# When the first loads start and how the last one arrives: two edits at the ends of a batched matrix product

## The chip, the core and the metric

The kernel runs on one core of a Trainium2 chip. The metric is device time in microseconds (us) for one execution; lower is better. The kernel before took 138.43 us (median of 4 runs, 138.32 to 138.64).

A core has a matrix engine (TensorE, PE in the profile), a vector engine (VectorE, DVE), a scalar engine (ScalarE, ACT), a general engine (GpSimd, POOL) and a synchronisation engine (SyncE, SP). Data moves between device memory and the core's own memory by DMA, on 16 DMA engines that all queues of the core share. A DMA is issued by an instruction of SyncE, ScalarE or GpSimd, and each of these three has a queue of its own: in the trace, queue 1 is SyncE's, queue 10 ScalarE's and queue 0 GpSimd's.

## The reference: what is computed

```python
a = randn(1024, 64, 64)   # float32
b = randn(1024, 64, 64)   # float32
out = matmul(a, b)        # float32, 1024 products of 64 x 64 matrices
```

The kernel reads 16.78 MB of a and as much of b, and writes 16.78 MB of output.

## The kernel before

The 1024 products are cut into 16 b tiles of 64 products (index t, 0 to 15) and 8 a tiles of 128 products (index s = t // 2, 0 to 7). The products are made in bf16 and summed in float32. Each a matrix must be transposed, and several small matrices are put into one 128 x 128 block for the matrix engine.

The work on a: `load_a(s)` (L62) issues four DMAs from GpSimd, one for each quarter h. They turn float32 into bf16 on the way: 512 KB are read and 256 KB written by each. `regroup(s)` (L76) reorders the tile on VectorE. `transpose(s, w)` (L83) makes 16 transposes on the matrix engine against the 128 x 128 tile `identity`, then copies them out of the accumulators, one half on VectorE (L94) and one on ScalarE (L96). `spread(t)` (L98) copies the blocks with four VectorE instructions into a block-diagonal tile, of which there are two, cleared once at the start (L164).

The work on b: `load_b(t)` (L70) issues one DMA of 1 MB for tiles 0 to 14, from ScalarE for t = 1 and 3, else from SyncE. `cast(t)` (L108) turns the tile into bf16 with one ScalarE instruction (L111). For the last tile, t = 15, there is no load into float32: `cast(15)` issues four GpSimd DMAs (L115) that turn float32 into bf16 on the way, 256 KB read and 128 KB written by each. The last b tile is called b15 from here on, the one before it b14.

The product: `multiply(t)` (L122) has four parts (gq). Each makes 16 matrix instructions (L144) and then copies one accumulator to the output tile, on ScalarE (L156), or for the last tile on VectorE where gq is odd (L154). `store(t)` (L118) issues the output's DMA from GpSimd: 1 MB in one piece (L134), but four pieces of 256 KB for the last tile (L128). It is called one step of the loop late (`HOLD = 2`), so that store(t - 1) stands behind multiply(t) in the order of the program.

The order of work on each engine is the order of the calls: the whole is under a manual schedule, and each engine runs its instructions as they are written, waiting where data or a buffer is missing. At the start:

```python
load_a(0)
for t in range(B_AHEAD):      # B_AHEAD = 4
    load_b(t)
...                           # two memsets
make_identity(nc, identity)   # two GpSimd instructions, after load_a(0)
for s in range(1, A_AHEAD):   # A_AHEAD = 3
    load_a(s)
```

`make_identity` is a library helper (masks.py): it fills the tile with zeros (a memset on GpSimd) and then writes ones on the diagonal (one GpSimd selection).

Buffers: three a tiles, four float32 b tiles, two of each working tile, five output tiles. Tile t of b therefore takes the buffer of tile t - 4 and waits for that tile's cast; a product waits for an output tile until the store five steps earlier has landed. At the end of each step of the loop come `cast(t + 1)`, `load_b(t + 4)` and `store(t - 1)` in this order, so GpSimd meets the four DMAs of `cast(15)` ahead of store 13.

Of the kernel before, what the change touches and what calls it, by code (L numbers as in the profile page):

```python
# [7 lines left out]

fp32 = mybir.dt.float32
# [4 lines left out]
def kernel(  # L14
# [3 lines left out]
    b: bass.AP,  # L18
    out: bass.AP,
):  # L20

# [3 lines left out]
    nc = tc.nc  # L28
# [4 lines left out]
    n_t, n_s = B // 64, B // 128  # L33
    A_AHEAD = 3
    B_AHEAD = 4
# [4 lines left out]
    b_v = b.rearrange("(t g h) (kp u) n -> t (h kp) g (u n)", h=4, g=16, u=2)  # L40
# [16 lines left out]
    ]  # L57
    identity = consts.tile([128, 128], bf16)
    a_tiles, b_tiles, abf_tiles, at_tiles, bbf_tiles = {}, {}, {}, {}, {}
    held = {}  # L60

    def load_a(s):  # L62
        a_sb = a_pool.tile([128, 4, 16, 64], bf16, name="a_sb")
        for h in range(4):
            nc.gpsimd.dma_start(  # L65
                out=a_sb[:, h, :, :].rearrange("p v k -> p (v k)"), in_=a_v[s, h]
            )
        a_tiles[s] = a_sb

    def load_b(t):  # L70
        b_sb = b_pool.tile([128, 16, 128], fp32, name="b_sb")
        queue = nc.scalar if t in (1, 3) else nc.sync
        queue.dma_start(out=b_sb[:], in_=b_v[t])  # L73
        b_tiles[t] = b_sb

    def regroup(s):  # L76
        a_sb = a_tiles.pop(s)
        a_bf = work.tile([128, 16, 4, 64], bf16, name="a_bf")
        nc.vector.tensor_copy(a_bf[:], a_sb[:].rearrange("p h v k -> p v h k"))  # L79
        abf_tiles[s] = a_bf  # L80
        at_tiles[s] = work.tile([128, 2, 2, 128, 8], bf16, name="at_sb")

    def transpose(s, w):  # L83
        a_cols = abf_tiles[s][:].rearrange("p v h k -> p v (h k)")
        for u in range(2):
            at_ps = t_psum.tile([128, 8, 128], bf16, name="at_ps")
            for vo in range(8):
                nc.tensor.transpose(  # L88
                    at_ps[:, vo, :], a_cols[:, 2 * vo + w, u::2], identity[:]
                )  # L90
            dst = at_tiles[s][:, w, u, :, :]
            src = at_ps[:].rearrange("p vo q -> p q vo")
            if u == 0:
                nc.vector.tensor_copy(dst, src)  # L94
            else:
                nc.scalar.copy(dst, src)  # L96

    def spread(t):  # L98
        at_v = at_tiles[t // 2][:].rearrange(
            "p w u (g mp) vo -> p (w u) g (mp vo)", g=32  # L100
        )
        half = slice(16 * (t % 2), 16 * (t % 2) + 16)
        bd_v = bd_tiles[t % N_BD][:].rearrange("p (wu g) h mo -> p wu g h mo", g=16)
        for h in range(4):
            rows = slice(32 * h, 32 * h + 32)
            nc.vector.tensor_copy(bd_v[rows, :, :, h, :], at_v[rows, :, half, :])  # L106

    def cast(t):  # L108
        b_bf = work.tile([128, 16, 128], bf16, name="b_bf")
        if t < n_t - 1:  # L110
            nc.scalar.copy(b_bf[:], b_tiles.pop(t)[:])  # L111
        else:
            for gq in range(4):
                rows = slice(4 * gq, 4 * gq + 4)
                nc.gpsimd.dma_start(out=b_bf[:, rows, :], in_=b_v[t, :, rows, :])  # L115
        bbf_tiles[t] = b_bf

    def store(t):  # L118
        for piece in held.pop(t):
            piece()  # L120

    def multiply(t):  # L122
        at_bd, b_bf = bd_tiles[t % N_BD], bbf_tiles.pop(t)
        last = t == n_t - 1
        o_sb = o_pool.tile([128, 4, 4, 2, 64], fp32, name="o_sb")

        def put(gq):
            nc.gpsimd.dma_start(  # L128
                out=o_v[t, :, 4 * gq : 4 * gq + 4, :],
                in_=o_sb[:, gq, :, :, :].rearrange("p g w n -> p (g w n)"),  # L130
            )

        def put_all():
            nc.gpsimd.dma_start(  # L134
                out=o_v[t], in_=o_sb[:].rearrange("p q g w n -> p (q g w n)")
            )

        for gq in range(4):
            o_ps = o_psum.tile([128, 4, 2, 64], fp32, name="o_ps")
            for g4 in range(4):  # L140
                g = 4 * gq + g4
                for w in range(2):
                    for u in range(2):
                        nc.tensor.matmul(  # L144
                            o_ps[:, g4, w, :],
                            at_bd[:, (2 * w + u) * 16 + g, :, :].rearrange(
                                "p h mo -> p (h mo)"
                            ),
                            b_bf[:, g, 64 * u : 64 * u + 64],
                            start=(u == 0),  # L150
                            stop=(u == 1),
                        )
            if last and gq % 2:
                nc.vector.tensor_copy(o_sb[:, gq, :, :, :], o_ps[:])  # L154
            else:
                nc.scalar.copy(o_sb[:, gq, :, :, :], o_ps[:])  # L156
        held[t] = [lambda q=q: put(q) for q in range(4)] if last else [put_all]

    with tc.manual_schedule():
        load_a(0)  # L160
        for t in range(B_AHEAD):
            load_b(t)
        for bd in bd_tiles:
            nc.vector.memset(bd[:], 0.0)  # L164
        make_identity(nc, identity)
        for s in range(1, A_AHEAD):
            load_a(s)
        regroup(0)
        transpose(0, 0)
        transpose(0, 1)  # L170
        spread(0)
        cast(0)
        regroup(1)
        load_a(A_AHEAD)
        transpose(1, 0)
        for t in range(n_t):
            s, half = t // 2, t % 2
            if t + 1 < n_t:
                spread(t + 1)
            if half == 0:  # L180
                if s + 2 < n_s:
                    regroup(s + 2)
                if s + 1 + A_AHEAD < n_s:
                    load_a(s + 1 + A_AHEAD)
            multiply(t)
            if t + 1 < n_t:
                cast(t + 1)
            if t + B_AHEAD < n_t - 1:
                load_b(t + B_AHEAD)
            if half == 0 and s + 1 < n_s:  # L190
                transpose(s + 1, 1)
            if half == 1 and s + 2 < n_s:
                transpose(s + 2, 0)
            if t >= HOLD - 1:
                store(t - HOLD + 1)
        for t in range(n_t - HOLD + 1, n_t):
            store(t)
# [30 lines left out]
```

## Time and profile before

| | |
|---|---|
| median of 4 runs | 138.43 us |
| the profiled execution | 138.32 us |
| its span, first to last instruction | 136.5 us |
| granted matrix clock, mean | 0.841 |
| queue 0 (GpSimd: a, stores, b15) | 25.69 MB, 70.4% of 16 engines' span |
| queue 1 (SyncE: b) | 13.63 MB, 28.4% |
| queue 10 (ScalarE: b1, b3) | 2.10 MB, 4.2% |
| b tiles from SyncE, issue to landing | 22.4 us, median |
| a quarters, issue to landing | 16.3 us, median |
| stores of 1 MB, issue to landing | 21.2 us, median |
| b15's pieces, issue to landing | 8.4 us, median |
| first regroup of a starts at | 16.77 us |
| last copy out of the accumulators starts at | 126.89 us |

All times within the profile count from the start of the span. The megabytes of a queue are counted on the writing side, so a load that turns float32 into bf16 counts for half of what it reads. The rows of a window of time give the busy time of PE, PEld (weight loads), DVE, ACT and POOL, each with its number of instructions, then the granted clock of the matrix engine, the mean busy share of the 16 DMA engines and the rate of their writes. A DMA share over 1 means that packets overlap on an engine. In the timeline each line has the start, the duration, the engine, the line of the kernel, the operation, what is written and read, and in brackets how long the engine had been idle and what ended that.

### The profile page before, as it was taken

The numbers are of one execution on the slowest core, as the hardware profiler recorded it, in microseconds if no ns is written. First come the engines' busy times: TensorE is split into PE (matmuls) and PEld (weight loads), VectorE is DVE, ScalarE is ACT, GpSimd is POOL, SyncE is SP. The second block draws the span as 40 slices with busy tenths as digits, with TensorE's granted clock in tenths as the row PEclk, the third lists the DMA queues.
The fourth block names the chain that finished last, engine by engine and source line by source line (L and its number), as shares of the span: only waits on it lengthen the run. The fifth ranks groups of instructions, "written<-read, shape, count | busy, mean of one in ns | idle before, by whom it ended". The sixth has DMA issues, their size and how long they took to land.

```text
span 136.5 us, 2992 instructions
## 1 busy us (share of the span) xinstructions
PE 58.8 (43%) x1280; PEld 56.5 (41%) x1280; DVE 83.7 (61%) x92; ACT 76.8 (56%) x96; POOL 47.3 (35%) x61
## 2 busy tenths in 40 slices
PE   0000073196854684470497206680085716078100
PEld 0000072195854684470497106580085715077100
DVE  5770067889699999998179803995058908802200
ACT  1120018158999999915976078830979767355100
POOL 6811142354245503451132734300203122914700
PEclk9999999658999999999658965899658996558965
DMA  2999999999999999999999999999999999999993
GB/s 86 305 304 311 304 275 259 209 246 274 242 251 290 378 283 269 331 380 366 279 269 353 376 360 271 269 369 383 382 380 379 383 384 383 377 246 312 295 282 97
DMA packets 19053, 41.61 MB, mean 305 GB/s; under 512 B 3168, under 2 KB 3168, under 8 KB 19040
## 3 DMA queue, kind: packets, MB, share of 16 engines
q0 software_dynamic: 11120, 25.69, 70.4%
q1 hardware_dynamic: 6864, 13.63, 28.4%
q10 hardware_dynamic: 1056, 2.10, 4.2%
q8 instruction: 10, 0.16, 0.5%
q14 instruction: 3, 0.02, 0.0%
HBM read 33.55 MB, written 16.78 MB: 369 GB/s over the span
## 4 chain that ended last, share of the span: by engine, by line
DMA 52%; SPq 12%; issue 9%; POOL 6%; ACT 6%; PE 5%; DVE 4%; POOLq 1%; DVEq 0%; ACTq 0%
DMA a_sb<-in_a_dram 21%; DMA b_sb<-in_b_dram 17%; DMA out_dram<-o_sb 15%; SPq L73 12%; ACT o_sb L156 3%; PE o_ps L144 3%; PE at_ps L88 3%; POOL b_bf L115 2%; DVE a_bf L79 2%; DVE at_bd L106 2%; POOL out_dram L134 2%; ACT at_sb L96 1%; POOL a_sb L65 1%; ACT b_bf L111 1%; POOL out_dram L128 1%
## 5 line engine op out<-in xcount | busy, mean ns | idle before, releaser
L144 PE MATMUL o_ps<-b_bf,at_bd 128*128 128x64 bf16 x1024 | 40.9, 208 | 44.9 <-ACT b_bf L111 44.4
L106 DVE COPY at_bd<-at_sb 32x2048 bf16<-32x2048 bf16 x64 | 46.0, 719 | 22.2 <-ACT at_sb L96 21.2
L144 PEld LDWEIGHTS <-at_bd 128*128 128x128 bf16 x1024 | 40.0, 108 | 46.7 <-issue 36.9
L156 ACT COPY o_sb<-o_ps 128x512 f32<-128x512 f32 x62 | 33.9, 620 | 22.1 <-DMA out_dram<-o_sb 15.5
L65 POOL DMA_DIRECT2D a_sb<-in_a_dram x32 | 20.6, 649 | 37.2 <-DMA a_sb<-in_a_dram 26.0
L134 POOL DMA_DIRECT2D out_dram<-o_sb x15 | 19.7, 1316 | 38.8 <-ACT o_sb L156 20.8
L111 ACT CAST b_bf<-b_sb 128x2048 bf16<-128x2048 f32 x15 | 29.1, 1943 | 4.9 <-DMA b_sb<-in_b_dram 4.9
L88 PE MATMUL at_ps<-identity,a_bf 128*128 128x128 bf16 x256 | 20.2, 244 | 23.2 <-DVE a_bf L79 23.2
L88 PEld LDWEIGHTS <-a_bf 128*128 128x128 bf16 x256 | 17.8, 111 | 23.4 <-DVE a_bf L79 23.4
L96 ACT COPY at_sb<-at_ps 128x1024 bf16<-128x1024 bf16 x16 | 16.9, 1054 | 17.2 <-PE at_ps L88 17.2
L94 DVE COPY at_sb<-at_ps 128x1024 bf16<-128x1024 bf16 x16 | 19.5, 1221 | 4.5 <-PE at_ps L88 4.4
L79 DVE COPY a_bf<-a_sb 128x4096 bf16<-128x4096 bf16 x8 | 10.3, 1294 | 7.6 <-DMA a_sb<-in_a_dram 7.4
L164 DVE MEMSET at_bd<- 128x4096 uint32 x2 | 6.9, 3472 | 2.5 <-PEq L212 1.7
L154 DVE COPY o_sb<-o_ps 128x512 f32<-128x512 f32 x2 | 1.4, 692 | 7.1 <-PE o_ps L144 7.1
L115 POOL DMA_DIRECT2D b_bf<-in_b_dram x4 | 3.3, 833 | 5.3 <-ACT o_sb L156 5.3
L96 ACT ACT_TABLE_LOAD x1 | 1.3, 1283 | 4.1 <-issue 4.1
L128 POOL DMA_DIRECT2D out_dram<-o_sb x4 | 3.0, 755 | 0.0
L73 ACT MOVE_SHAPE b_sb<-in_b_dram x2 | 0.6, 320 | 1.6 <-issue 0.9
masks.py:199 POOL TENSOR_SCALAR_AFFINE_SELECT identity<-identity 128x128 bf16<-128x128 bf16 x1 | 0.3, 289 | 0.1
masks.py:197 POOL MEMSET identity<- 128x128 bf16 x1 | 0.3, 267 | 0.0
L212 POOL MEMSET const-float32-0.0<- 128x1 f32 x1 | 0.1, 99 | 0.2 <-issue 0.2
L212 POOL MEMSET const-bfloat16-1.0<- 128x1 bf16 x1 | 0.1, 102 | 0.0
(2 smaller groups left out, 0.2 us busy)
## 6 DMA issues: line engine op xcount, KB each, us to landing
out_dram<-o_sb POOLq DMA_DIRECT2D x15, 1024.0 KB, 21.2
a_sb<-in_a_dram POOLq DMA_DIRECT2D x32, 256.0 KB, 16.3
out_dram<-o_sb POOLq DMA_DIRECT2D x4, 256.0 KB, 6.9
b_bf<-in_b_dram POOLq DMA_DIRECT2D x4, 128.0 KB, 8.4
b_sb<-in_b_dram SPq DMA_DIRECT2D x13, 0.5 KB, 22.4
b_sb<-in_b_dram ACTq DMA_DIRECT2D x2, 0.5 KB, 18.2
```

What stands on the lines that cost most here:

```text
L65: nc.gpsimd.dma_start(out=a_sb[:, h, :, :].rearrange("p v k -> p (v k)"), in_=a_v[s, h])
L73: queue.dma_start(out=b_sb[:], in_=b_v[t])
L79: nc.vector.tensor_copy(a_bf[:], a_sb[:].rearrange("p h v k -> p v h k"))
L88: nc.tensor.transpose(at_ps[:, vo, :], a_cols[:, 2 * vo + w, u::2], identity[:])
L94: nc.vector.tensor_copy(dst, src)
L96: nc.scalar.copy(dst, src)
L106: nc.vector.tensor_copy(bd_v[rows, :, :, h, :], at_v[rows, :, half, :])
L111: nc.scalar.copy(b_bf[:], b_tiles.pop(t)[:])
L134: nc.gpsimd.dma_start(out=o_v[t], in_=o_sb[:].rearrange("p q g w n -> p (q g w n)"))
L144: nc.tensor.matmul(o_ps[:, g4, w, :], at_bd[:, (2 * w + u) * 16 + g, :, :].rearrange("p h mo -> p (h mo)"), b_bf[:, g, 64 * u : 64 * u + 6 ...
L156: nc.scalar.copy(o_sb[:, gq, :, :, :], o_ps[:])
L164: nc.vector.memset(bd[:], 0.0)
```

## The change

The change has two edits.

At the start, the fill of `identity` with zeros moves into `load_a(0)`, between the first of its four DMAs and the second. The loads of b tiles 0 and 1 get an added dependency on that fill, so that SyncE and ScalarE issue them after it; b tiles 2 and 3 stand behind them on the same two engines. The selection that writes the diagonal stays where it was, now written out instead of in the helper.

At the end, `load_b` is called for t = 15 as for the others, so that b15 is loaded in float32 by SyncE, into the buffer of tile 11. Its cast to bf16 is done in four instructions of 512 columns each: parts 0 and 2 on ScalarE, parts 1 and 3 on VectorE. The four GpSimd DMAs of `cast(15)` are gone.

```diff
     def load_a(s):
         a_sb = a_pool.tile([128, 4, 16, 64], bf16, name="a_sb")
         for h in range(4):
+            if s == 0 and h == 1:
+                begun.append(nc.gpsimd.memset(identity[:], 0.0))
             nc.gpsimd.dma_start(
                 out=a_sb[:, h, :, :].rearrange("p v k -> p (v k)"), in_=a_v[s, h]
             )
...
         queue = nc.scalar if t in (1, 3) else nc.sync
-        queue.dma_start(out=b_sb[:], in_=b_v[t])
+        load = queue.dma_start(out=b_sb[:], in_=b_v[t])
+        if t < 2:
+            tc.add_manual_dep(
+                load.ins,
+                begun[0].ins.name,
+                mybir.DependencyInfo(
+                    mybir.DependencyClass.Sync, mybir.DependencyReason.DATA
+                ),
+                reason="first load of a goes ahead",
+            )
...
         b_bf = work.tile([128, 16, 128], bf16, name="b_bf")
+        b_sb = b_tiles.pop(t)
         if t < n_t - 1:
-            nc.scalar.copy(b_bf[:], b_tiles.pop(t)[:])
+            nc.scalar.copy(b_bf[:], b_sb[:])
         else:
             for gq in range(4):
                 rows = slice(4 * gq, 4 * gq + 4)
-                nc.gpsimd.dma_start(out=b_bf[:, rows, :], in_=b_v[t, :, rows, :])
+                if gq % 2:
+                    nc.vector.tensor_copy(b_bf[:, rows, :], b_sb[:, rows, :])
+                else:
+                    nc.scalar.copy(b_bf[:, rows, :], b_sb[:, rows, :])
...
-        make_identity(nc, identity)
+        nc.gpsimd.affine_select(
+            out=identity[:],
+            in_=identity[:],
+            compare_op=mybir.AluOpType.not_equal,
+            fill=1.0,
+            base=0,
+            pattern=[[-1, 128]],
+            channel_multiplier=1,
+        )
...
-            if t + B_AHEAD < n_t - 1:
+            if t + B_AHEAD < n_t:
                 load_b(t + B_AHEAD)
```

More of the change, by code (lines that the diff above doesn't have):

```diff
@@ L5 @@
 from concourse import bass_utils, mybir
-from concourse.masks import make_identity
 from concourse._compat import with_exitstack
@@ L59 @@
     a_tiles, b_tiles, abf_tiles, at_tiles, bbf_tiles = {}, {}, {}, {}, {}
-    held = {}
+    held, begun = {}, []
     def load_a(s):
```

## The prediction

> **What bounds the kernel now.** I read the page's slices first. The DMA row stands at 9 from the second slice to the last but one: the sixteen DMA engines, not a compute engine, are full for the whole run.
>
> ```profile
> span 136.5 us, 2992 instructions
> PE 58.8 (43%) x1280; PEld 56.5 (41%) x1280; DVE 83.7 (61%) x92; ACT 76.8 (56%) x96; POOL 47.3 (35%) x61
> DMA  2999999999999999999999999999999999999993
> HBM read 33.55 MB, written 16.78 MB: 369 GB/s over the span
> ```
>
> Then busy time by window (the last two columns are the DMA share and GB/s counted on the writing side), at the start and at the end, where the change acts.
>
> ```profile
> 0.00:2.39 2.39, 0.00 (x0) 0.00 (x0) 0.72 (x1) 0.64 (x2) 1.30 (x6) 1.00 0.00 0
> 2.39:4.76 2.37, 0.00 (x0) 0.00 (x0) 2.37 (x1) 0.00 (x0) 2.30 (x7) 1.00 0.96 310
> 4.76:16.00 11.24, 0.00 (x0) 0.00 (x0) 3.85 (x2) 1.28 (x1) 3.17 (x6) 1.00 1.08 303
> ...
> 96.00:108.00 12.00, 7.12 (x155) 7.00 (x155) 6.70 (x9) 11.02 (x16) 2.31 (x2) 0.72 1.03 381
> ...
> 117.50:119.50 2.00, 0.00 (x0) 0.00 (x0) 1.58 (x3) 1.15 (x1) 2.00 (x3) 0.50 1.03 387
> 119.50:126.00 6.50, 5.34 (x112) 4.97 (x111) 0.62 (x1) 3.68 (x6) 1.59 (x3) 0.67 1.36 280
> ...
> 128.00:134.00 6.00, 0.00 (x0) 0.00 (x0) 0.00 (x0) 0.00 (x0) 0.94 (x2) 0.72 0.99 281
> ```
>
> Nothing moves before 2.39. With b loads and stores mixed, 381 GB/s pass. From 128 to 134 only stores are left, and they pass at 281, although stores alone ran at 387 for the short stretch from 117.5. The last 10 us are thus a drain of finished output: the compute engines are done at 127.6.
>
> Last the timeline, which gives the order of issue at both ends.
>
> ```profile
> 0.79 0.85 ACTq L73 DMA_DIRECT2D b_sb<-in_b_dram  x1
> 0.80 2.49 SPq L73 DMA_DIRECT2D b_sb<-in_b_dram  x2
> 1.30 2.33 POOL L65 DMA_DIRECT2D a_sb<-in_a_dram  x4 [0.85 <-POOLq L212]
> ...
> 3.57 0.27 POOL masks.py:197 MEMSET identity<- 128x128 bf16 x1
> ...
> 115.31 3.30 POOL L115 DMA_DIRECT2D b_bf<-in_b_dram  x4 [5.31 <-ACT o_sb L156]
> ...
> 118.35 1.90 ACT L111 CAST b_bf<-b_sb 128x2048 bf16<-128x2048 f32 x1 [2.99 <-DMA b_sb<-in_b_dram]
> 118.61 1.27 POOL L134 DMA_DIRECT2D out_dram<-o_sb  x1
> ...
> 124.79 1.16 POOL L134 DMA_DIRECT2D out_dram<-o_sb  x1 [4.91 <-ACT o_sb L156]
> 125.94 2.99 POOL L128 DMA_DIRECT2D out_dram<-o_sb  x4
> ```
>
> I also counted the trace's DMA packet records by queue and size: 2048 B on queue 1 (SyncE) and 10 (ScalarE) are b, 2048 B on queue 0 (GpSimd) are a (4096 B read each), 4096 B on queue 0 are stores, 256 B on queue 0 are the last b tile (b15; tiles and stores are numbered from 0). The first packet of b comes at 2.39; queue 1 then runs alone, 342 packets, until queue 0 (4.76) and queue 10 (4.87) start together.
>
> **The Trainium skill.** "DMA: Bandwidth & Descriptors", section "Issuing engines are not separate DMA queues", says that loads of all issuers share the same engines and interleave; "Queues, rings and completion order" says that an engine takes turns between queues packet by packet. The trace agrees: around 113 both queues pass 31 or 32 packets each in 0.5 us. It disagrees for 2.39 to 4.76, where one queue held all engines. The section "Latency and other measured facts" gives 0.6 us to the first byte from SyncE and about 1 us from GpSimd; here SyncE took 2.39 − 0.80 = 1.6 us. "ScalarE: Activation LUTs", section "What ACT_TABLE_LOAD costs", prices an operation with immediate scale and bias at 186 + 0.833 N ns; for N = 2048 that is 1892 ns, and the cast row has 1943.
>
> **The change, part by part.**
>
> *Head: the identity fill moves behind the first of a's four issues, and the first two b loads wait for it.* a's first issue ends at 1.30 + 2.33/4 = 1.88, the fill at 2.15 (its 0.27). SyncE and ScalarE then issue at about 2.3, 1.5 us later, with their second loads (b2, b3) behind them; behind those stand on ScalarE only the table load (6.42) and the first copy of transposed a at 19.98, so twelve microseconds cover it. Moving the fill delays a's other three issues by 0.27, hidden by the 1.2 us that the first piece's 128 packets need. b's first packet comes at 2.3 + 1.6 = 3.9. The unknown is a's first packet. Lower end 2.4: store 14 (issue 124.79 to 125.95) must have had packets moving by 126.5, when store 13's were used up, so a warm issue needs at most about 0.5 us past its end, 1.88 + 0.5. Upper end 4.76, where it is now. I take 2.9, because the two queues that started together at 4.8 look held off by queue 1, not slow by themselves. Bytes read by 4.76: now 342 x 2048 = 0.70 MB. After: 1.0 us of a alone at 434 GB/s (around 24.5 the count shows 53 packets of 4096 B in 0.5 us) and 0.86 us at 400 GB/s (the 4.76 to 16.00 mix: 303 plus the second half of a's reads, 517 x 2048 B over 11.24 us) = 0.78 MB. That is 0.08 MB ahead, at 381 GB/s: **−0.2 us**. With a at 4.76: 0.86 us of b alone = 0.29 MB, 0.41 behind: +1.1 us.
>
> In the likely case a's first tile has 109 of its 512 packets before b begins. If b then holds the engines for another 2.4 us, the other 403, at the present pace of 517 in 11.24 us, end at 6.3 + 8.8 = 15.1 instead of 16.0; without that hold, at 12.7. I take a **lead of 1.0 us** for the first regroup (now 16.77) and what follows. It buys no time by itself while the DMA is full, but moves each b load, which waits for a cast, up in its queue.
>
> *Tail: the last tile of b goes through SyncE.* Removed: four GpSimd issues (3.30 us) and 2048 packets of 256 B. In the 7.0 us from 119.5 to 126.5 they shared the engines with 346 stores (3204 to 3550). Those alone, at 47 in 0.5 us (count at 118 to 119.5), take 3.68 us; the small packets cost 3.3. Added: 512 packets of 2048 B in queue 1. In the mix 32 of them ride with 32 stores in 0.5 us, of which the stores need 0.34; so 512 cost 512/32 x 0.16 = 2.6 us. **−0.75 us.** The issue stands behind b14's (SyncE is done at 102.47) and waits for the cast of tile 11 (97.51 to 99.4): no stall.
>
> Store 13 no longer stands behind GpSimd's 3.30 us: it goes at 115.4, not 118.61, which feeds queue 0 while queue 1 works. Queue 1 ran dry at 117.5; with b15 it goes on for 8.0 us (64 packets of both kinds in 0.5 us) to 125.5, and stores reach 3063 + 512 = 3575, where store 13 ends at 3584. Store 14 is issued at 124.79 and flows by 126.5. So the DMA could stand idle up to 0.9 us there; the lead of 1.0 brings b14 and store 14 forward as well as b15, while stores done by then are fewer, and closes the gap. I take **+0.1**, ends 0 and 0.9.
>
> Without reads beside them, stores slow from 47 to 35 in 0.5 us, 0.0037 us each. Left over after the last read: now 575 (at 126.0), after about 521 + 64 = 585: **+0.1**, ends −0.2 and +0.4.
>
> *Casts.* b15 lands 0.7 us after its last packet (as b14: 117.6, landed 118.27), at 126.2, or 125.2 with the lead. Two ScalarE casts of 512 cost 0.6 us each (0.59 for a copy of that width, 613 ns by the price above). VectorE's lie between 0.3 (no such row) and the 0.69 of its 512-wide copy; it is idle then. Matrix work for four parts at the present 0.7 us a part, the last copy at 130.9, the last issue to 131.7, its 64 packets to 133.1. The drain lasts to about 134, so this is hidden by 0.9 us even without the lead; without that cover each microsecond of cast would count in full.
>
> Sum: −0.2 − 0.75 + 0.1 + 0.1 = −0.75. The profiled execution took 138.32, 1.8 outside its span of 136.5 and 0.11 under the median of 138.43. From the median: 137.7, a span of about 135.75.
>
> **Rivals.** Measurement tells 0.2% (0.28 us) from no change.
>
> 1. *The gap at store 14 eats the gain*: no lead, so b15 and store 13 end together at 125.5 and store 14 flows at 126.5 as now; from there 512 stores remain both before and after. −0.2 − 0.75 + 0.9: 138.4. For it: that equality, and that clock throttling set multiply 14's pace. Against it: a's early start should move all of it.
> 2. *Slower: the DMA stands idle at the start.* If a's first packet needs its present 4.76 whatever b does, only b runs from 3.9, 0.41 MB are lost, and a's first tile comes no earlier. +1.1 − 0.75, with the store gap (0 to 0.9) half open: +0.8, 139.2. It outweighs the tail's gain once a's first packet is later than about 3.7 (0.75 us is 0.29 MB). For it: 1.88 to 4.76 is a long way if the queue was free. Against: queue 10, issued at 0.79, started at the same moment.
> 3. *a holds the engines as b did*, its whole first tile passes early, the lead is 4 us or more, and the small packets cost more than counted: about 136.5.
>
> **The numbers.** Forecast 0.45, first rival 0.20, second 0.30, third 0.05. The forecast's own range is 136.9 to 138.1. For eight in ten the range takes in rival 1 and most of rival 2: 136.8 to 139.5. Faster by over 0.2%: nearly all of the forecast, the third, a quarter of rival 1, 0.49; within: 0.20; slower: 0.31.
>
> **What would show it.** Right: queue 0's first packet near 2.9 and ahead of queue 1's at 3.9, the first regroup near 15.8, no 256 B packets, queue 1's last at 124.5, a DMA share without a dip around 125, stores alone again at about 281 GB/s. Wrong: no packet before 3.9; b or a holding the engines alone for long; a dip before store 14; the last store's issue later than 132, when the chain through b15's casts would set the end.

## The result and the profile after

| | before | after |
|---|---|---|
| median | 138.57 us (55 runs, 138.13 to 138.93) | 138.75 us (35 runs, 137.75 to 139.73) |
| ratio of the times, with its 95% interval | | 1.0022 [1.0011, 1.0033] |
| the profiled execution | 138.32 us | 138.10 us |
| its span | 136.5 us | 136.3 us |
| its granted matrix clock | 0.841 | 0.861 |

The kernel became slower by 0.2%: 0.3 us by the ratio, while the medians lie 0.18 us apart. A gain of 0.75 us had been forecast. It also became uneven: its runs spread over 2.0 us, those of before over 0.8 us. All ratios here leave out executions over 1.5% above the fastest of the same kernel, which concerns e11 alone (five of its 22). The profiled execution is the second fastest of the changed kernel's 36, so it shows where bytes are lost and won back, but not why a typical execution takes 0.6 us more. The page of the changed kernel, its head and the two new rows of casts:

```profile
span 136.3 us, 2995 instructions
...
DMA  2999999999999999999999999999999999999992
...
HBM read 33.55 MB, written 16.78 MB: 369 GB/s over the span
...
L126 DVE CAST b_bf<-b_sb 128x512 bf16<-128x512 f32 x2 | 0.8, 423 | 6.1 <-DMA b_sb<-in_b_dram 6.1
...
L128 ACT CAST b_bf<-b_sb 128x512 bf16<-128x512 f32 x2 | 1.1, 616 | 2.0 <-DMA b_sb<-in_b_dram 2.0
```

The DMA still stands at 9 throughout and the mean rate is the same 369 GB/s: a slice of 3.4 us is too coarse for what happened. The windows of the changed kernel, with the columns as before:

```profile
0.00:2.69 2.69, 0.00 (x0) 0.00 (x0) 1.02 (x1) 0.02 (x1) 1.60 (x8) 1.00 0.02 1
2.69:4.00 1.31, 0.00 (x0) 0.00 (x0) 1.31 (x1) 0.62 (x1) 1.26 (x3) 1.00 1.01 95
4.00:6.33 2.33, 0.00 (x0) 0.00 (x0) 1.53 (x2) 0.00 (x0) 2.33 (x6) 1.00 1.11 198
...
23.20:28.00 4.80, 2.65 (x34) 2.65 (x35) 2.81 (x3) 0.73 (x1) 1.71 (x2) 1.00 1.10 300
...
119.50:124.30 4.80, 2.96 (x57) 2.86 (x55) 0.00 (x0) 2.35 (x4) 0.82 (x1) 0.72 1.03 382
124.30:127.00 2.70, 1.26 (x25) 1.25 (x25) 0.76 (x2) 1.35 (x3) 0.34 (x1) 0.75 1.04 388
...
128.00:134.00 6.00, 1.26 (x25) 1.14 (x22) 1.03 (x2) 0.59 (x1) 2.69 (x4) 0.78 0.93 283
```

Three of the same windows in the kernel before, at the head and at the end of the first b loads:

```profile
2.69:4.00 1.31, 0.00 (x0) 0.00 (x0) 1.31 (x1) 0.00 (x0) 1.24 (x4) 1.00 0.97 322
4.00:6.33 2.33, 0.00 (x0) 0.00 (x0) 1.53 (x2) 0.00 (x0) 2.33 (x5) 1.00 1.05 300
...
23.20:28.00 4.80, 1.22 (x12) 1.23 (x13) 3.60 (x6) 1.25 (x1) 2.50 (x4) 0.67 1.13 210
```

The rate counts the writing side, so where only a flows the memory is read at twice the figure. From 2.69 to 4.00 a alone wrote 95 GB/s, thus read 190, where b alone had read 322. The DMA share is 1.01 all the same: the engines count as busy, with packets that take long. From 4.00 to 6.33 a alone read 2 x 198 = 396. From 23.2 to 28 the kernel before had a alone (210 written, 420 read); the changed one has a mix there. At the end the dip to 280 from 119.5 to 126, which the 256 B packets made, is gone (382 and 388), and the last stores pass at 283 as before at 281.

The timeline of the changed kernel:

```profile
1.29 0.69 POOL L65 DMA_DIRECT2D a_sb<-in_a_dram  x1 [0.84 <-POOLq L233]
1.98 0.22 POOL L64 MEMSET identity<- 128x128 bf16 x1
2.29 0.86 ACTq L73 DMA_DIRECT2D b_sb<-in_b_dram  x1
2.30 5.55 SPq L73 DMA_DIRECT2D b_sb<-in_b_dram  x2
...
13.12 1.23 DVE L88 COPY a_bf<-a_sb 128x4096 bf16<-128x4096 bf16 x1 [3.71 <-DMA a_sb<-in_a_dram]
...
115.16 1.23 POOL L147 DMA_DIRECT2D out_dram<-o_sb  x1 [3.42 <-ACT o_sb L169]
...
123.48 1.15 POOL L147 DMA_DIRECT2D out_dram<-o_sb  x1 [7.09 <-ACT o_sb L169]
125.02 0.76 DVE L126 CAST b_bf<-b_sb 128x512 bf16<-128x512 f32 x2 [6.05 <-DMA b_sb<-in_b_dram]
125.07 1.14 ACT L128 CAST b_bf<-b_sb 128x512 bf16<-128x512 f32 x2 [1.99 <-DMA b_sb<-in_b_dram]
125.74 3.51 PE L157 MATMUL o_ps<-b_bf,at_bd 128*128 128x64 bf16 x64 [3.29 <-ACT b_bf L128]
...
130.47 0.75 POOL L141 DMA_DIRECT2D out_dram<-o_sb  x1 [0.34 <-issue]
```

The wait does what it says: SyncE and ScalarE issue b at 2.3. The packet records add what the timeline can't show. a's first packet comes at 2.69, but only 62 packets start from 2.5 to 4.0, at 440 to 455 ns each in the first microsecond, where 173 ns is usual. b's first packets come at 6.33 (queue 1) and 6.86 (queue 10), 4.0 and 4.6 us after their issue. It is not the load of a that is slow by nature: in the kernel before its first 16 packets, which started at 4.76 beside b, took 178 ns, and in the changed kernel b's first 16, beside a, took 96 and 84 ns. What is slow is the start of a into engines that have done nothing yet. The first regroup starts at 13.12, 3.65 us earlier than before.

To weigh one stage against another, a ledger: the bytes read and written by each moment, as the difference to the kernel before, turned into time at 381 GB/s (e1 to e12 are explained in the next section):

| us ahead of before (minus: behind) at | 5 | 12 | 24 | 28 | 40 | 116 | 120 | 124 | 128 |
|---|---|---|---|---|---|---|---|---|---|
| after | -0.54 | -0.60 | -0.55 | -0.79 | -0.81 | -0.74 | -0.72 | -0.40 | +0.10 |
| e1_tail_only | -0.23 | -0.24 | -0.26 | -0.28 | -0.30 | -0.28 | -0.25 | +0.07 | +0.13 |
| e2_head_only | -0.55 | -0.60 | -0.60 | -0.80 | -0.87 | -0.78 | -1.04 | -1.84 | -1.79 |
| e3_no_wait | -0.26 | -0.25 | -0.27 | -0.31 | -0.31 | -0.27 | -0.27 | +0.02 | +0.06 |
| e8_wait_fourth | -0.55 | -0.46 | -0.44 | -0.65 | -0.83 | -0.71 | -0.69 | -0.38 | -0.14 |
| e9_warm | -0.22 | -0.23 | -0.22 | -0.25 | -0.27 | -0.28 | -0.23 | +0.08 | +0.01 |
| e10_after_warm | -0.59 | -0.74 | -0.72 | -0.95 | -0.98 | -0.90 | -0.86 | -0.55 | -0.15 |
| e12_all_sync | -0.31 | -0.28 | -0.35 | -0.54 | -0.75 | -0.69 | -0.61 | -0.33 | -0.02 |

One warning about its zero line. Eight of the kernels below issue b without a wait and in the old order (e1, e3, e4, e5, e6, e7, e9, e11), and all eight stand at -0.23 to -0.27 at 12 us. So the profiled execution of before had a start that was a quarter of a microsecond better than usual. The head edit itself falls behind by the rest: 0.35 us by 12 us (0.2 in e8, 0.5 in e10), and another 0.2 between 24 and 40.

And one warning about its reach. A deficit in the middle is not yet lost time. e12 stands at -0.69 at 116, nearly as low as the changed kernel, and has the lowest median of all. The changed kernel's own profiled execution is level with e1 again at 128 (+0.10 and +0.13), while its stores run at their full rate for longer. In e8 and e10, which have the wait and whose profiled executions lie near their medians, -0.14 and -0.15 are left at 128. So the ledger shows where the head edit falls behind; it does not show how much of that a typical execution of the changed kernel loses in the end.

### The profile page after: what moved, and what is told of

Its sections match the earlier page's. It is cut to its first block, busy times and chain, and to the rows that moved or that the text cites. A ratio compares the mean times of both kernels' runs of the same rounds, so it can differ in the third digit from the quotient of the medians.

```text
span 136.3 us, 2995 instructions
## 1 busy us (share of the span) xinstructions
PE 61.0 (45%) x1280; PEld 58.9 (43%) x1280; DVE 85.0 (62%) x94; ACT 78.0 (57%) x98; POOL 43.9 (32%) x57
## 4 chain that ended last, share of the span: by engine, by line
DMA 57%; issue 27%; POOL 11%; POOLq 1%
DMA a_sb<-in_a_dram 39%; DMA out_dram<-o_sb 18%; POOL out_dram L147 6%; POOL a_sb L65 3%; POOL out_dram L141 2%; POOLq L244 1%; POOL identity L178 0%; POOL identity L64 0%; POOLq L147 0%; POOLq L178 0%; POOLq L141 0%; POOLq L65 0%; POOLq L233 0%
## 5 line engine op out<-in xcount | busy, mean ns | idle before, releaser
L157 PE MATMUL o_ps<-b_bf,at_bd 128*128 128x64 bf16 x1024 | 42.3, 212 | 46.4 <-ACT b_bf L121 34.6
L157 PEld LDWEIGHTS <-at_bd 128*128 128x128 bf16 x1024 | 41.7, 111 | 48.0 <-issue 36.6
L115 DVE COPY at_bd<-at_sb 32x2048 bf16<-32x2048 bf16 x64 | 46.6, 727 | 19.6 <-ACT at_sb L105 18.5
L97 PE MATMUL at_ps<-identity,a_bf 128*128 128x128 bf16 x256 | 20.9, 248 | 21.9 <-DVE a_bf L88 21.8
L97 PEld LDWEIGHTS <-a_bf 128*128 128x128 bf16 x256 | 18.4, 114 | 22.3 <-DVE a_bf L88 22.3
L126 DVE CAST b_bf<-b_sb 128x512 bf16<-128x512 f32 x2 | 0.8, 423 | 6.1 <-DMA b_sb<-in_b_dram 6.1
L128 ACT CAST b_bf<-b_sb 128x512 bf16<-128x512 f32 x2 | 1.1, 616 | 2.0 <-DMA b_sb<-in_b_dram 2.0
```

The costliest lines, as they stand in the source:

```text
L97: nc.tensor.transpose(at_ps[:, vo, :], a_cols[:, 2 * vo + w, u::2], identity[:])
L157: nc.tensor.matmul(o_ps[:, g4, w, :], at_bd[:, (2 * w + u) * 16 + g, :, :].rearrange("p h mo -> p (h mo)"), b_bf[:, g, 64 * u : 64 * u + 6 ...
```

## The experiments

The theory after the result: the head edit is what costs, because the engines do less in the first microseconds and nothing later gives it back; the tail edit gains what it was said to gain. The rivals: the tail's gain is eaten at the end (by the chain of casts and products, by stores that slow down, by the late store 14), or the moved fill costs and not the wait. Times are medians; ratios are to the kernel before on the same chip.

**e1_tail_only and e2_head_only: one edit each.** e1 is the kernel before with the tail half of the diff, e2 the kernel before with the head half, both as shown above.

> The kernel before with the second edit alone (b15 loaded by SyncE, cast in four parts). Theory 1 (ledger of bytes: the head edit loses 0.55 to 0.75 us of DMA time, the tail edit gives 0.75 back): ratio to the kernel before 0.9955 (0.6 us faster, 0.993 to 0.997), b15 landed near 126, last store packets near 134. Theory 2 (a gap before store 14 eats the tail's gain when a's lead is missing): ratio 0.999 to 1.001, with a dip of the store packets near 125.5 to 126.5. Theory 3 (the later landing of b15 costs, the head is free): slower, 1.002 or more.

Measured: 138.04 us, ratio 0.9954 [0.9935, 0.9973]: the tail alone gains 0.64 us (0.0046 x 138.74, the median of before on that chip).

> The kernel before with the first edit alone (fill of the identity after a's first issue, first two b loads wait for it). Theory 1: slower by 0.55 to 1.0 us, ratio 1.004 to 1.008; the bytes read and written lag by about 0.28 MB from 4 us to the end of the loads. Theory 2: the first tile of a is early and the lead pays: 0.998 to 1.000. Theory 3 (the head is free): 0.999 to 1.001.

Measured: 140.61 us, ratio 1.0137 [1.0114, 1.0159]: the head alone costs 1.9 us, where 0.55 to 1.0 was expected. In the company of the tail edit it costs less: 1.0022 / 0.9954 = 1.0068, 0.94 us, with an interval of about 0.3 either way. The ledger says where the difference arises: e2 stands where the changed kernel stands until 116, and loses another 1.1 us from there to 124. Its windows and its timeline at that place:

```profile
118.00:121.50 3.50, 3.15 (x63) 2.99 (x58) 1.40 (x2) 2.07 (x4) 0.93 (x1) 0.51 1.02 312
121.50:126.00 4.50, 0.00 (x0) 0.00 (x0) 0.00 (x0) 0.27 (x1) 1.16 (x1) 0.88 1.32 175
```

```profile
114.52 3.15 POOL L124 DMA_DIRECT2D b_bf<-in_b_dram  x4 [2.80 <-ACT o_sb L165]
...
117.66 1.26 POOL L143 DMA_DIRECT2D out_dram<-o_sb  x1
...
127.04 3.57 PE L153 MATMUL o_ps<-b_bf,at_bd 128*128 128x64 bf16 x64 [5.89 <-DMA b_bf<-in_b_dram]
```

With the lead, queue 1 runs dry at 115.2. b15's four DMAs are issued at 114.5 but stand in queue 0 behind stores; their first packets come at 121.8. Meanwhile the stores are alone: 2.6 us at full rate, then at 312. After that the 256 B packets are alone, at 175, and the product starts at 127.04. So the lead that the head edit buys does harm with the old tail: queue 1 ends earlier, and more of b15 and of the stores pass with nothing beside them.

**e3_no_wait: the changed kernel without the added dependency.** The fill stays where the change put it.

```diff
-        if t < 2:
+        if False:
             tc.add_manual_dep(
```

> The changed kernel without the added dependency: the fill of the identity stays behind a's first issue, the b loads wait for nothing. If the wait is what the head edit costs, it equals the kernel with the tail edit alone (theory 1: 0.9955; theory 2: 0.999 to 1.001), its first b packet comes at 2.4 and a's at 4.8. If the moved fill itself costs, it stays near the changed kernel, 1.002.

Measured: 138.27 us, ratio 0.9981 [0.9962, 1.0000]. The changed kernel stands at 1.0022 / 0.9981 = 1.0041 of it, 0.57 us slower, some 0.3 either way. b's first packet is back at 2.4, a's at 5.0, and the ledger is that of e1. So it is mainly the wait, not the moved fill, that costs. e3 lies 0.27% above e1, though, about as much either way: a small cost of the moved fill is not excluded.

**e4_tail_one_cast: e1 with the cast of b15 in one piece.** It asks whether the cast is covered.

```diff
-        b_sb = b_tiles.pop(t)
-        if t < n_t - 1:
-            nc.scalar.copy(b_bf[:], b_sb[:])
-        else:
-            for gq in range(4):
-                rows = slice(4 * gq, 4 * gq + 4)
-                if gq % 2:
-                    nc.vector.tensor_copy(b_bf[:, rows, :], b_sb[:, rows, :])
-                else:
-                    nc.scalar.copy(b_bf[:, rows, :], b_sb[:, rows, :])
+        nc.scalar.copy(b_bf[:], b_tiles.pop(t)[:])
```

> The kernel before with b15 loaded by SyncE, but cast by one ScalarE instruction of 2048 columns as the other tiles are. It ends 1.9 us after b15's landing instead of 0.65 us for the first part. If the drain of stores hides the chain cast, product, copy, store (as the prediction counted): the same as with four parts, 0.994 to 0.997. If that chain sets the end in some or all executions: 0.5 to 1.3 us slower than that, 0.999 to 1.005.

Measured: 139.87 us, ratio 1.0066 [1.0041, 1.0092], 1.0066 / 0.9954 = 1.0113 of e1: 1.55 us. Its timeline, and one of its windows:

```profile
127.02 1.90 ACT L110 CAST b_bf<-b_sb 128x2048 bf16<-128x2048 f32 x1 [1.90 <-DMA b_sb<-in_b_dram]
128.96 3.57 PE L139 MATMUL o_ps<-b_bf,at_bd 128*128 128x64 bf16 x64 [4.47 <-ACT b_bf L110]
...
133.74 0.75 POOL L123 DMA_DIRECT2D out_dram<-o_sb  x1 [0.40 <-issue]
```

```profile
131.00:132.00 1.00, 1.00 (x23) 1.00 (x21) 0.56 (x1) 0.28 (x1) 0.81 (x2) 0.50 0.10 29
```

From landing to product it took 1.94 us instead of 0.72 in e1, so 1.2 us more, and in the time 1.55 us came out, some 0.3 either way. (In this execution b15 also landed 1.0 us later than in e1's, 127.0 against 126.0, which the edit doesn't explain; so the two timelines differ by more than the edit.) The DMA stood at a share of 0.10 from 131 to 132: store 14 was used up before the first piece of store 15 was there. For comparison the timeline of e1 at the same place:

```profile
126.03 0.76 DVE L117 CAST b_bf<-b_sb 128x512 bf16<-128x512 f32 x2 [7.19 <-DMA b_sb<-in_b_dram]
...
126.75 3.57 PE L148 MATMUL o_ps<-b_bf,at_bd 128*128 128x64 bf16 x64 [3.22 <-ACT b_bf L119]
...
131.54 0.75 POOL L132 DMA_DIRECT2D out_dram<-o_sb  x1 [0.40 <-issue]
```

Its last store is issued at 131.54, and the last packet ends at 134.5. In e4 the same step is 133.74 and 136.55. From the issue of the last 256 KB to the end of its last packet it takes 2.8 to 3.0 us even with the engines nearly free. In e1, then, the chain of cast, product, copy and store ends about when the drain of the stores does.

**e5_reverse: the kernel before with the tiles in reverse order of place.** It computes the same products, last tile first, and asks whether the slow last stores belong to a place in memory. The same turn of the index in the other places is left out here.

```diff
-                out=a_sb[:, h, :, :].rearrange("p v k -> p (v k)"), in_=a_v[s, h]
+                out=a_sb[:, h, :, :].rearrange("p v k -> p (v k)"), in_=a_v[n_s - 1 - s, h]
...
-        queue.dma_start(out=b_sb[:], in_=b_v[t])
+        queue.dma_start(out=b_sb[:], in_=b_v[n_t - 1 - t])
...
-                out=o_v[t], in_=o_sb[:].rearrange("p q g w n -> p (q g w n)")
+                out=o_v[n_t - 1 - t], in_=o_sb[:].rearrange("p q g w n -> p (q g w n)")
```

> The kernel before with the tiles taken in reverse order (products 1023 to 0), so that the last tile worked on is tile 0 of the output. Question: why do the last two stores pass at 281 GB/s and the one before at 387? If the slow drain belongs to stores that run with no reads beside them, the last 500 packets again take 0.22 to 0.24 us each and the ratio is 0.999 to 1.001. If it belongs to the place of the last tiles in device memory, the last stores take 0.174 us and the kernel is about 1.5 us faster, 0.988 to 0.991, with slow stores early instead.

Measured: 138.52 us, ratio 0.999 [0.9974, 1.0007]; the last stores again pass at 288 GB/s from 128 to 134, 198 to 241 ns a packet. The slow drain belongs to the end of the run, not to the end of the output.

**e6_split_b15 and e7_obuf4: two ways to relieve the end.** e6 is e1 with the load of b15 in four DMAs, so that the first cast can start earlier; e7 is e1 with four output tiles instead of five, to change how many stores are left when the reads end.

```diff
-        queue.dma_start(out=b_sb[:], in_=b_v[t])
+        if t < n_t - 1:
+            queue.dma_start(out=b_sb[:], in_=b_v[t])
+        else:
+            for gq in range(4):
+                rows = slice(4 * gq, 4 * gq + 4)
+                queue.dma_start(out=b_sb[:, rows, :], in_=b_v[t, :, rows, :])
```

> The tail edit alone, with b15's load cut into four SyncE DMAs of 256 KB, one for each part of the cast; parts land about 2 us apart, so three of the four casts, products and copies come before the last landing. Chain theory: the last stores are issued 1 to 2 us earlier, the executions near 138.8 of the tail edit vanish, ratio 0.990 to 0.994. Drain theory: the DMA is full to the end anyway, ratio as the tail edit, 0.994 to 0.997. If four issues cost SyncE's queue its place: 0.998 or more.

Measured: 138.94 us, ratio 1.0013 [1.0000, 1.0026]; e1's gain is gone. The four parts land at 123.98, 127.99, 128.72 and 129.41, where the whole tile landed at 126.0 in e1. The packet records show why: a quarter has 2 KB in each partition instead of 8 KB, and its packets have 512 B instead of 2048 B, 2048 of them instead of 512. They went nearly one for one with the stores all the same: from 118 to 121 some 90 packets of b15 and 80 of stores a microsecond, where in e1 some 65 packets of 2048 B went with 61 stores. So b15 moved a third of the bytes that it moved in e1. The page "Perfetto Trace Analysis" of the Trainium skill, section "DMA Optimizations", offers splitting where the DMA engines are generally idle; here they are full, and the last part landed 3.4 us later.

```diff
-    o_pool = ctx.enter_context(tc.tile_pool(name="o_pool", bufs=5))
+    o_pool = ctx.enter_context(tc.tile_pool(name="o_pool", bufs=4))
```

> The tail edit alone with four output tiles instead of five, so that at most four stores can be behind when the reads end. If a store with no reads beside it costs 0.0037 us more, and some 100 to 250 fewer are left (613 with five tiles): 0.4 to 0.9 us faster than the tail edit, 0.989 to 0.993. If the fourth tile's wait stalls ScalarE and with it the casts and the loads of b: slower than the tail edit, 0.998 or more.

Measured: 138.65 us, ratio 0.9987 [0.9970, 1.0004]. The stores left at 126.0 were 579 against 574 in e1, so the edit didn't change what it was to change. It decides nothing.

**e8_wait_fourth: the changed kernel with the fill, and so b's issue, behind the fourth issue of a.** If b only had to let a fixed number of a's packets pass, its first packet would come at 6.3 to 6.6 as in the changed kernel; if a load that is issued beside a running queue needs a time of its own, b comes about 4 us after its issue.

```diff
         for h in range(4):
-            if s == 0 and h == 1:
-                begun.append(nc.gpsimd.memset(identity[:], 0.0))
             nc.gpsimd.dma_start(
...
             )
+        if s == 0:
+            begun.append(nc.gpsimd.memset(identity[:], 0.0))
```

> The changed kernel with the fill of the identity behind a's fourth issue instead of its first; the b loads are issued at about 4.0 instead of 2.3. If the queue that comes first passes about 21 packets on each engine before another gets a turn, b's first packet comes at 6.3 to 6.6 as in the changed kernel and the time stays within 0.2% of it (ratio 1.000 to 1.005). If a b load has its own delay of 4 us from issue to first packet, it comes at 8, with a's 512 packets of the first tile near their end, and the kernel is some 0.2 to 0.5 us slower still, 1.005 to 1.01.

Measured: 138.64 us, ratio 0.9994 [0.9986, 1.0002]. That is 0.4 us faster than the changed kernel (0.9994 / 1.0022, about 0.2 either way), where 0.2 to 0.5 us slower was expected if the load has a time of its own, and its runs spread over 0.65 us only. Its timeline:

```profile
3.92 6.24 SPq L73 DMA_DIRECT2D b_sb<-in_b_dram  x2
...
10.80 1.23 DVE L88 COPY a_bf<-a_sb 128x4096 bf16<-128x4096 bf16 x1 [1.39 <-DMA a_sb<-in_a_dram]
...
129.52 0.75 POOL L141 DMA_DIRECT2D out_dram<-o_sb  x1 [0.28 <-issue]
```

b was issued at 3.92 and its first packet came at 8.2, 4.3 us later. The time is the load's own. And although b came 1.9 us later than in the changed kernel, the ledger at 12 us is better, -0.46 against -0.60: once a's packets are quick, a alone reads faster than the mix. A late b by itself loses no bytes here. What the ledger loses it loses in the first microseconds, while a starts up (0.188 MB read by 4.0, where e1 has 0.340), and between 24 and 40.

**e9_warm, e10_after_warm and e11_warm2: the matrix engine kept busy before the last product.** 24 products of the identity with itself, which nothing uses, stand ahead of tile 15's product in e1 (e9) and in the changed kernel (e10), and ahead of tiles 14 and 15 in e1 (e11).

```diff
+            if t == n_t - 1:
+                warm(24)
             multiply(t)
```

`warm` makes the products, into an accumulator that nothing reads.

> The tail edit alone, with 24 products of the identity by itself (results not used) on the matrix engine between the products of tile 14 and those of tile 15, so that its clock is not at half when b15 lands. If the chain landing of b15, cast, product at half clock (3.57 us), copy, store sets the end in the slower executions of the tail edit (137.5 to 139.0): products in about 2.1 us, the last store issued about 1 us earlier, the executions near 138.8 gone, median 137.5 to 137.8, ratio 0.991 to 0.994. If the drain sets the end: 0.994 to 0.997 and the same spread. If the extra products come late and stand in the way of tile 15: slower than the tail edit.

Measured: 138.34 us, ratio 0.9972 [0.9957, 0.9986]. Its timeline:

```profile
127.03 2.03 PE L159 MATMUL o_ps<-b_bf,at_bd 128*128 128x64 bf16 x64 [1.97 <-ACT b_bf L119]
...
128.59 2.98 POOL L143 DMA_DIRECT2D out_dram<-o_sb  x4 [2.69 <-ACT o_sb L171]
```

The same microsecond in e1 and then in e9:

```profile
127.00:128.00 1.00, 1.00 (x23) 1.00 (x21) 0.00 (x0) 0.42 (x2) 0.00 (x0) 0.50 1.01 328
```

```profile
127.00:128.00 1.00, 0.97 (x34) 0.97 (x34) 0.07 (x1) 0.81 (x2) 0.00 (x0) 1.00 1.01 315
```

The last product took 2.03 us instead of 3.57. The page "TensorE: Matmul & The Clock Gate" of the Trainium skill, section "What's actually happening", says that the array falls to half its clock after an idle window of about 3.4 us; the granted clock of 0.50 from 127 to 128 in e1 and of 1.00 in e9 agrees. But GpSimd then issues the four pieces back to back (2.98 us). The last one goes at 130.8 instead of 131.5, and the stores drain at the same pace: the last packet ends at 134.65, in e1 at 134.52. The chain is shorter and the time isn't.

> The changed kernel with the same 24 extra products. The ledger theory says that the head edit loses 0.7 us of DMA time whatever the end looks like: ratio 0.5% (0.7 us) above that of the tail edit with the extra products, 0.996 to 0.999. If the head edit's cost lies in the chain at the end: both the same within 0.2%.

Measured: 138.47 us, ratio 0.9994 [0.9978, 1.0009]. Against e9, 0.9994 / 0.9972 = 1.0022, about 0.002 either way: with the extra products, the head edit costs 0.3 us. Against the changed kernel e10 is 0.4 us faster (0.9994 / 1.0022, about 0.3 either way), and its runs spread over 1.0 us instead of 2.0. So the chain of the last product seems to cost something in the changed kernel, in its slower executions, although the profiled one has cover for it. e8, whose last store goes 0.95 us earlier, gains as much, which fits.

> The tail edit alone with 24 extra products before tile 14 as well as before tile 15. Store 14 is issued up to 1.3 us earlier (124.56 with the tail edit), which closes the dip of store packets at 125.5 to 126.5. Chain theory: as with one set of extra products or 0.1 to 0.3 us faster, 0.989 to 0.993. Drain theory: no difference to the tail edit, 0.994 to 0.997.

Measured: 138.39 us, ratio 0.9971 [0.9953, 0.9989], from 137.51 to 140.04. In its profiled execution b15 landed at 127.27, 2.2 us after its last packet, where 0.7 is usual. Such a late landing could be why several kernels with the tail edit spread so widely, since everything at the end waits for it. But one profile shows it once, and e6 and e8 have the tail edit too and spread over 0.5 and 0.65 us; it isn't settled.

**e12_all_sync: e1 with b1 and b3 issued by SyncE too.** Only one b queue then runs beside a, not two, so a gets more of the engines, and with it a lead without any wait.

```diff
-        queue = nc.scalar if t in (1, 3) else nc.sync
+        queue = nc.sync
```

> The tail edit alone, with b1 and b3 from SyncE as well, so that only two queues share the engines at the start and a's first tile gets half of the packets instead of a third, with no wait added. Ledger theory: no DMA time is lost at the start (b's first packet at 2.4, a's at 4.8, bytes by 12 us within 0.1 MB of the kernel before), the first regroup starts at about 13.4 as in the changed kernel, b15 lands about 1 us earlier than with the tail edit alone (126.0): ratio 0.990 to 0.995. Rival: the earlier start only leaves more stores for the slow stretch after the last read (749 in the changed kernel, 613 with the tail edit alone): 0.995 to 0.999.

Measured: 137.90 us, ratio 0.9941 [0.9918, 0.9965]. It is the best version found, 0.8 us under the kernel before and 1.1 us under the changed one by the ratios, but not to be told from e1. Its timeline:

```profile
0.80 15.28 SPq L73 DMA_DIRECT2D b_sb<-in_b_dram  x4
...
14.27 1.23 DVE L79 COPY a_bf<-a_sb 128x4096 bf16<-128x4096 bf16 x1 [4.86 <-DMA a_sb<-in_a_dram]
```

The first regroup comes 2.5 us earlier than before. In the ledger it stands with e1 until 12, since the start is the old one, and then loses 0.4 us from 24 to 40, as the changed kernel does, although no wait was added. That loss goes with the lead, not with the wait, and it isn't seen in the time.

## Why the prediction was wrong

Forecast: 137.7 us, faster by over 0.2%. Measured: slower by 0.22%. The time lies within the stated range; the direction is the other one.

**The step that failed** is the head's sum: "After: 1.0 us of a alone at 434 GB/s ... and 0.86 us at 400 GB/s ... = 0.78 MB. That is 0.08 MB ahead, at 381 GB/s: -0.2 us." By 4.76 the changed kernel had read 0.483 MB, the profiled execution before 0.70 and e1, which starts as usual, 0.600. So in place of 0.2 us ahead it was 0.3 us behind a usual start. The sum's two inputs failed differently.

- *The rate of a's first packets.* 434 GB/s was read from a running queue at 24.5. Into engines at rest a read 190 GB/s from 2.69 to 4.00. This is the mis-sized term: 1.31 us at 434 would have been 0.57 MB, and 0.25 MB came (62 packets of 4096 B); the missing 0.32 MB are 0.83 us at 381 GB/s. The step "I take 2.9" came out, with 2.69, in part by luck: the reason given was that queue 1 held a off. The moment of the first packet was not the whole question.
- *"b's first packet comes at 2.3 + 1.6 = 3.9."* It came at 6.33. The 1.6 us was the start of a load into engines at rest, applied to one that starts beside a running queue. The trace of before had held the right price: b1, issued at 0.79 beside SyncE's load, moved at 4.87 (4.1 us), and b4, issued at 24.54 beside a, at 28.5 (4.0 us). The text even noticed the common start at 4.8 and put it down to queue 1 holding the engines, against the turns by packet; e8 shows that the time is the load's own, so there was nothing yet to take turns with. By itself this cost no bytes, as e8's ledger shows, but it made the lead of the first regroup 3.65 us instead of "a lead of 1.0 us". That b15 then landed 1.0 us before e1's (125.0 and 126.0) is the forecast size by luck.

**"It buys no time by itself while the DMA is full"** failed too. Full engines aren't equally fast: from 23.2 to 28 a alone read 420 GB/s before, where the mix after reads about 400 (in 0.5 us some 48 packets of b of 2048 B and 25 of a of 4096 B), and the lead does away with most of the stretch in which a was alone. That is the second deficit of the ledger, 0.2 us in the changed kernel and 0.4 in e12. Whether it costs time is not shown: e12 has it and the lowest median.

The head was thus forecast at -0.2. By the ratios it is +0.94 with the changed tail (against e1), +0.57 against e3 and +0.3 with the extra products (e10 against e9). Its size between 0.3 and 0.9 stays open, its sign doesn't. That the wait costs is shown by taking it out (e3). That the slow first packets put the kernel 0.3 us behind by 5 us is shown by four profiles (the changed kernel, e2, e8, e10). That this deficit is what lengthens a typical execution is argued: it fits e10 against e9, where 0.16 us of it are left at 128 and the last packet ends 0.34 us later, but the profiled execution of the changed kernel makes it good.

**The tail was right in direction and size, in part by luck.** Its own terms were -0.75, +0.1 and +0.1, together -0.55; e1 measured -0.64, with -0.9 to -0.4 as its interval. But the +0.1 for the gap counted on the lead, which e1 doesn't have; without it the prediction allowed up to +0.9. b15 with the lead was to land at 125.2 and landed at 125.00; store 13 went at 115.16 for 115.4; the casts took 616 ns for 613 on ScalarE and 423 ns on VectorE, within the bounds of 0.3 to 0.69.

**The gap at store 14**: with the lead it closed (388 GB/s from 124.3 to 127.0), as forecast. Without it, in e1, the DMA share fell to 0.81:

```profile
125.20:126.50 1.30, 0.00 (x0) 0.00 (x0) 0.47 (x2) 0.41 (x1) 0.52 (x1) 0.50 0.81 303
```

At 303 instead of 388 GB/s that is 0.22 of 1.3 us, 0.3 us. The first rival had the mechanism, at three times its price. One reason lies in its sum: 3063 is the count of stores at 118.0. At 117.5, where its 8.0 us begin, it was 3016, so store 13 had packets left when b15 ended; in e1 some 110.

**The slow last stores**: 585 were forecast to be left after the last read; it was about 750 in the changed kernel, since reads ended at 124.4. It hardly mattered in its profiled execution: the first of them still passed at full rate, and 283 GB/s from 128 on is the pace of before.

**The casts "hidden by 0.9 us"** weren't: with the old head, 1.2 us more of cast cost 1.55 us (e4). The failed term is "the last issue to 131.7, its 64 packets to 133.1", 2.15 us from the issue's start to the last packet; it took 2.8 to 3.0 in e1 and e4. In the changed kernel the last issue is at 130.47, and there a cover of about 1.3 us is real in the profiled execution, though e10 suggests that it doesn't reach in all.

**The rivals.** The second, an under-used DMA at the start, is what happened in kind, and its net +0.8 compares with a measured +0.3. But it put the loss down to a's packets starting late; they started early and slowly. The third had the lead (over 3.6 us, a holding the engines alone) and drew the opposite conclusion from it. No profile of a typical, slower execution of the changed kernel exists, so why its median lies 0.6 us over its profiled execution is not shown. By e10 the chain of the last product has a share in it; what delays it in some executions stays open. In e9 and e11, without the head edit, the shorter chain made neither the time nor the spread smaller to speak of.

## What to carry to other kernels

Price the start of a transfer by the state in which it starts: into engines at rest, beside a running queue, and its first packets apart from the rest, since full engines are not equally fast engines. Where the DMA is the bound, sum the bytes of both kernels by time: such a ledger shows at once which stage falls behind and how much one profiled execution differs from the next. Follow it to the end, for what is won back there was not lost: e12 and the changed kernel stand alike at 116, and their times differ by 1.1 us. Try two edits apart before trusting their sum: here the head cost 1.9 us with the old tail, 0.9 us with the new one and 0.3 us once the last product was quicker.

## What the runs showed of the hardware

- A load of b that was issued beside another queue's load had its first packet 3.7 to 4.6 us later (b1 and b4 before, both b loads after and in e2, b in e8), and a's first from GpSimd, before, 3.5 us later (1.30 to 4.76). With nothing else issued before it took 1.6 us from SyncE (0.80 to 2.39) and 1.4 us from GpSimd (1.29 to 2.69 after). The cause is open.
- The first packets into engines at rest were slow: 440 to 455 ns instead of 173 for a after, from 2.5 to 3.5, and 254 ns instead of about 90 for b in e1, from 2.0 to 2.5. A load that started beside a running one was quick from its first packets (a before 178 ns, b after 84 to 96). The cause is open, also of why a suffered longer.
- Stores alone kept their full rate (174 ns a packet, 388 GB/s) for a while after the last read and then fell to 200 to 250 ns (281 GB/s before, 283 after, 276 in e1, 288 in e5, from 128 to 134). The full rate lasted about 3 us in the changed kernel and in e2, 2.5 us in e8, and about 1 us in e1. It isn't the place in memory (e5); what it is stays open.
- A tile cut into four loads had packets of a quarter of the size, 512 B for 2048 B. They still went nearly one for one with the stores, so the tile's bytes came at a third of the rate (e6, from 118 to 121).
